# Modulation vectors of a two-block kernel: from multiply-adds on three engines to plain fp32 matmuls in four 32-column parts

## The chip, the cores and the metric

One Trainium2 chip, one NeuronCore, one launch. The metric is device microseconds of the launch; the kernel before took 2239.73 us (median of 3 runs, 2230.85 to 2242.94). The engines have separate instruction queues that run in order: PE (TensorE), DVE (VectorE), ACT (ScalarE), POOL (GpSimd) and SP, which here issues nearly all DMAs. SP's queue is in order too: a DMA that waits for its buffer holds up every DMA behind it.

## What is computed

The input runs through two layers of a first block (four mixer branches, gates, a feed-forward part) and then through two layers of a second block (attention, gating, convolution, a feed-forward part with 22 tiles of 128 hidden units). Each layer `l` of the second block needs six modulation rows of 1024 numbers, for the latent stream (from `c`) and for the context stream (from `c_ctx`):

```python
def adaln(cvec, w, b, n):
    m = jax.nn.silu(cvec) @ w[:, : n * D_MODEL] + b[: n * D_MODEL]
    return jnp.split(m, n, axis=-1)

cmod = adaln(c_ctx, w_mod[l], b_mod[l], 2 if last else 6)
...
sh1, sc1, g1, sh2, sc2, g2 = [m[:, None, :] for m in adaln(c, w_mod[l], b_mod[l], 6)]
```

`w_mod[l]` is 1024 x 6144 in fp32, 25.2 MB a layer. It depends on nothing that the blocks compute, so it may be done at any time before its layer. In the last layer the context stream needs two of the six rows only.

## The kernel before

The large projections are done as three fp32r matmuls each (`mm3`, L509 to L511): weights are loaded as 512 KB units into a ring of six buffers (`RAW = 6`, tag "raw", L262), split by ACT into `hi` (L275) and by DVE into `lo` (L278), at most four split units ahead of PE (`HL = 4`).

The modulation vectors are made by a generator, `mods(l)`, that is advanced in small steps by `fill(n)` beside other work. A step takes one unit of 512 KB of `w_mod`: two slabs of 128 rows by 512 columns. There are 48 steps a layer: six rows `r`, two halves `h` of 512 columns, four pairs of slabs. The units are loaded on SP (L1133) into the same ring of six buffers as the other weights, one unit ahead (`WM_AHEAD = 1`).

In a step each slab is multiplied by one number per partition of silu(c) (and of silu(c_ctx) where that is needed) and added to an accumulator `macc` of 128 x 512. The first slab is written by ACT (L1151). For the latent stream DVE does a fused multiply-add (L1156). For the context stream ACT multiplies the slab in place (L1153) and POOL adds it (L1154). After four steps the 128 partitions of `macc` are summed by PE with a one-hot stationary operand `pick` (L1164): plain fp32, four matmuls per stream, each on a 32-column part of the array, with 128 moving columns. DVE copies the sums out of PSUM (L1167), PE transposes them (L1169), DVE adds the bias (L1171). For rows 2 and 5 the resulting columns are written to DRAM from POOL's queue with 4-byte elements (L1175, tile `md`), and read back later as rows (L1180).

The steps are taken in five stages: 16 in the gate part of the first block's layer 0 (one in every second gate unit), 22 in its feed-forward part (one per hidden tile), 10 in the feed-forward part of the first block's layer 1, and for the second layer's vectors 33 and 15 in the two parts of the feed-forward of the second block's layer 0 (three per hidden tile, 512 tokens). The order of instructions on each engine is fixed when the program is made, by a list scheduler that goes by priorities in program order and a timeline of its own; buffers are packed into memory by the same program.

Of the kernel before, what the change touches and what calls it, by code (L numbers as in the profile page):

```python
# [9 lines left out]
F32 = mybir.dt.float32  # L10
FR = mybir.dt.float32r
AF = mybir.ActivationFunctionType
# [17 lines left out]
KEEP = 962 + 4 + 2 * (280 + 80 + 96 + 48)  # L30
# [268 lines left out]
class Kern:  # L299
# [8 lines left out]
    MPOOL = (1,)  # L308
# [14 lines left out]
    WM_AHEAD = 1  # L323
# [7 lines left out]
    def __init__(self, nc, tc, ctx, dr, stop=None):  # L331
# [15 lines left out]
        self.ident, cst, self.tabs, self.pick, self.ct, self.ones, self.nh, self.par_f = (  # L347
            self.keep(n) for n in (128, cpk.n, 512, 64, 16, 1, 1, 240))
# [246 lines left out]
    # ---------------------------------------------------------------- first block  # L595
# [515 lines left out]
    # ---------------------------------------------------------------- second block  # L1111
    def mods(self, l):
        nc, dr = self.nc, self.dr
        if l == 0:
# [12 lines left out]
        units = [(r, h, k) for r in range(6) for h in range(2) for k in range(0, 8, 2)]  # L1127
        loaded = []

        def load():  # L1130
            r, h, k = units[len(loaded)]
            wm = self.wp.tile([128, UNIT], F32, tag="raw", name=f"wm{l}_{r}_{h}_{k}", bufs=self.RAW)
            nc.sync.dma_start(wm, dr["w_mod"][l, r, h, k // 2])  # L1133
            loaded.append(wm)

        for i, (r, h, k0) in enumerate(units):
# [3 lines left out]
            if h == 0 and k0 == 0:  # L1140
                col = self.keep(16).rearrange("p (w m) -> p w m", w=2)
                self.mcol[l, r] = col
            if k0 == 0:
                acc = self.slot("macc")
            for k in (k0, k0 + 1):
                w = loaded[i][:, 512 * (k - k0):512 * (k - k0) + 512]
                for which in range(nw):
                    c = self.ct[:, 2 * k + which:2 * k + which + 1]
                    dst = acc[:, 512 * which:512 * which + 512]
# [7 lines left out]
            if k0 < 6:  # L1157
                yield
                continue
# [640 lines left out]
```

## Time and profile before

| | |
|---|---|
| median of 3 runs | 2239.73 us |
| profiled execution: span | 2238.6 us |
| mean granted TensorE clock | 0.973 |
| PE busy (matmul records) | 2101.8 us, 94% |
| DVE / ACT / POOL busy | 1575.9 / 1175.6 / 681.8 us |
| DMA read from HBM | 361.8 MB, mean 163 GB/s |

The page is of one execution. PE's busy time is a union of matmul records, whose ends are modelled and overlap, so 94% hides slow stretches: in a stretch without waits 256-column fp32r matmuls start 0.12 us apart though each record lasts 0.28 us. What the modulation steps cost is read by setting stages with such steps beside equal stages without, and by the waits inside them. A plain fp32 matmul has two records on PE.

### The profile page before, as it was taken

To read this page: it belongs to the slowest core of one execution; us is meant where nothing else is said; L and a number is where in the kernel's file an instruction comes from. 1 tells how busy PE (TensorE), PEld (TensorE's weight loads), DVE (VectorE), ACT (ScalarE), POOL (GpSimd) and SP (SyncE) were. 2 spreads that over 40 slices of the span, in tenths; PEclk is the share of its full clock that TensorE was granted. 3 is DMA by queue.
4 is the path that set the end of the run, shared out by engine and by line. 5 is a ranking of instruction groups with operands and counts; after the bars stand their busy time and mean duration, and the time that the engine had idled before them with its cause. 6 is when DMAs were issued, how large, how long until landed. Compare 5 with 4: busy or idle time off the path is not lost.

```text
span 2238.6 us, 34899 instructions
## 1 busy us (share of the span) xinstructions
PE 2101.8 (94%) x13152; PEld 1824.3 (81%) x13152; DVE 1575.9 (70%) x2594; ACT 1175.6 (53%) x2084; POOL 681.8 (30%) x564
## 2 busy tenths in 40 slices
PE   8999999976999999999897997998989999899999
PEld 7788898876888888998887886686778888678997
DVE  8757788856669566758985569779856635976664
ACT  6456756645554555556665455556323334465552
POOL 2102243556513100212545217109411221721330
PEclk9999999988999999999998999899999999999999
DMA  7545566676755444456567654245745722324553
GB/s 269 182 139 164 158 206 207 192 145 213 232 184 179 160 134 140 141 180 207 171 139 154 235 169 149 78 149 172 204 150 179 170 85 85 113 85 142 182 195 113
DMA packets 102552, 366.70 MB, mean 164 GB/s; under 512 B 12752, under 2 KB 12912, under 8 KB 102384
## 3 DMA queue, kind: packets, MB, share of 16 engines
q1 hardware_dynamic: 99920, 358.65, 52.1%
q0 software_dynamic: 2464, 5.83, 1.0%
q8 instruction: 103, 1.69, 0.3%
q14 instruction: 65, 0.53, 0.1%
HBM read 361.76 MB, written 2.68 MB: 163 GB/s over the span
## 4 chain that ended last, share of the span: by engine, by line
PE 72%; DVE 13%; DMA 5%; issue 5%; POOL 4%; ACT 2%; SPq 0%; DVEq 0%; POOLq 0%; ACTq 0%
PE mm L509 21%; PE mm L510 21%; PE mm L511 21%; DMA wm<-in_w_mod 4%; DVE lo L278 4%; DVE cv L1482 3%; POOL macc L1154 3%; DVE macc L1156 2%; PE ax L1292 1%; ACT hi L275 1%; PE ax L932 1%; PE ax L891 1%; DMA raw<-in_w_f 1%; PE ax L1320 1%; PE ax L890 1%
## 5 line engine op out<-in xcount | busy, mean ns | idle before, releaser
L278 DVE TENSOR_TENSOR lo<-raw,hi 128x1024 fp32r<-128x1024 f32 (+2 forms) x552 | 741.5, 1346 | 379.4 <-ACT hi L275 376.4
L275 ACT ACTIVATE hi<-raw 128x1024 fp32r<-128x1024 f32 (+1 forms) x564 | 593.2, 1053 | 620.7 <-PE mm L510 252.6
L509 PE MATMUL mm<-hThi,hi 128*128 128x256 f32 (+1 forms) x2408 | 730.2, 305 | 8.7 <-DVE gz L1271 2.9
L511 PE MATMUL mm<-hThi,lo 128*128 128x256 f32 (+1 forms) x2408 | 724.3, 302 | 9.1 <-DVE lo L278 9.1
L510 PE MATMUL mm<-hTlo,hi 128*128 128x256 f32 (+1 forms) x2408 | 727.3, 303 | 0.5 <-DVE hTlo L472 0.5
L509 PEld LDWEIGHTS mm<-hThi,hi 128*128 128x128 f32 x2408 | 466.2, 194 | 40.6 <-issue 13.1
L511 PEld LDWEIGHTS mm<-hThi,lo 128*128 128x128 f32 x2408 | 466.7, 194 | 26.2 <-DVE lo L278 9.3
L510 PEld LDWEIGHTS mm<-hTlo,hi 128*128 128x128 f32 x2408 | 467.9, 194 | 17.3 <-issue 3.3
L1154 POOL TENSOR_TENSOR macc<-macc,wm 128x512 f32<-128x512 f32 x112 | 191.2, 1708 | 179.7 <-ACT wm L1153 170.3
L1156 DVE SCALAR_TENSOR_TENSOR macc<-wm,kept,macc 128x512 f32<-128x512 f32 x168 | 182.8, 1088 | 70.1 <-DMA wm<-in_w_mod 57.4
L510 PE MATMUL mm<-lo,hThi 128*128 128x512 f32 (+2 forms) x480 | 182.1, 380 | 9.7 <-DVE lo L278 9.7
L509 PE MATMUL mm<-hi,hThi 128*128 128x512 f32 (+2 forms) x480 | 181.7, 386 | 5.5 <-DVE rb L580 3.1
L511 PE MATMUL mm<-hi,hTlo 128*128 128x512 f32 (+2 forms) x480 | 180.2, 378 | 0.0
L509 PE MATMUL mm<-hi,hh 128*128 128x512 f32 x440 | 172.4, 392 | 0.0
L510 PE MATMUL mm<-lo,hh 128*128 128x512 f32 x440 | 172.0, 391 | 0.0
L511 PE MATMUL mm<-hi,hl 128*128 128x512 f32 x440 | 171.7, 391 | 0.0
L839 POOL TENSOR_TENSOR th<-th,gh 128x512 f32<-128x512 f32 (+1 forms) x44 | 54.4, 1237 | 262.6 <-DVE th L1533 262.6
L1153 ACT ACTIVATE wm<-wm,kept 128x512 f32<-128x512 f32 x112 | 80.1, 721 | 77.0 <-DVE macc L1156 74.3
L510 PEld LDWEIGHTS mm<-lo,hThi 128*128 128x128 f32 x480 | 90.9, 190 | 27.9 <-DVE lo L278 12.4
L509 PEld LDWEIGHTS mm<-hi,hThi 128*128 128x128 f32 x480 | 90.8, 190 | 27.7 <-issue 8.5
L511 PEld LDWEIGHTS mm<-hi,hTlo 128*128 128x128 f32 x480 | 90.4, 189 | 16.6 <-issue 0.7
L511 PEld LDWEIGHTS mm<-hi,hl 128*128 128x128 f32 x440 | 83.0, 189 | 17.6
(354 smaller groups left out, 3189.2 us busy)
## 6 DMA issues: line engine op xcount, KB each, us to landing
raw<-in_w_f SPq DMA_DIRECT2D x364, 512.0 KB, 4.1
raw<-in_w_s SPq DMA_DIRECT2D x190, 512.0 KB, 3.5
wm<-in_w_mod SPq DMA_DIRECT2D x96, 512.0 KB, 4.3
bc<-csd POOLq DMA_DIRECT2D x32, 128.0 KB, 4.3
mrow<-md SPq DMA_DIRECT2D x6, 512.0 KB, 3.9
row<-in_rows SPq DMA_DIRECT2D x4, 512.0 KB, 4.9
raw<-in_w_f SPq DMA_DIRECT2D x4, 510.0 KB, 4.7
par<-in_par_s SPq DMA_DIRECT2D x2, 918.5 KB, 8.0
```

Of the source, the lines that this page charges most:

```text
L275: nc.scalar.activation(hi[:, :n], raw[:, :n], AF.Copy)
L278: ins = eng.tensor_sub(lo[:, :n], raw[:, :n], hi[:, :n].bitcast(F32)).ins
L509: nc.tensor.matmul(ps, ah, bh, start=first, stop=False)
L510: nc.tensor.matmul(ps, ah, bl, start=False, stop=False)
L511: nc.tensor.matmul(ps, al, bh, start=False, stop=last)
L839: nc.gpsimd.tensor_mul(tt, tt, gh)
L890: nc.tensor.matmul(ps[:, 0:128], q[:, :128], k[:, :128], start=True, stop=True)
L891: nc.tensor.matmul(ps[:, 128:384], q[:, 128:], k, start=True, stop=True)
L1153: nc.scalar.activation(w, w, AF.Copy, scale=c)
L1154: nc.gpsimd.tensor_add(dst, dst, w)
L1156: nc.vector.scalar_tensor_tensor(dst, w, c, dst, op0=ALU.mult, op1=ALU.add)
L1482: nc.vector.scalar_tensor_tensor(c, y[:, j:j + 256], wj, c, op0=ALU.mult, op1=ALU.add)
```

## The change

`mods` no longer multiplies on DVE, ACT and POOL. A padded stationary operand `ctp` (128 x 32 for each of eight 128-row blocks, silu(c) and silu(c_ctx) in columns 0 and 1, zeros in the rest) is made once. `w_mod` is laid out on the host as units of 128 rows x 1024 columns of one row `r`: still 48 units of 512 KB a layer, one per (`r`, 128-row block `k`). Every second step (`MSTEP = 2`) PE does two blocks: for each, four plain fp32 matmuls with 256 moving columns, one on each 32-column part of the array, all accumulating in one PSUM tile over the eight blocks. Then ACT copies 128 x 256 out, PE transposes twice, DVE adds the bias to eight columns at once. The units have a ring of their own of four buffers (tag "wm", `WM = 4`), and are loaded two steps ahead. Rows 2 and 5 are still written to DRAM from POOL's queue, now with one DMA of 1024 4-byte elements per stream instead of two of 512.

```diff
-            nc.gpsimd.memset(self.pick, 0.0)
-            nc.gpsimd.memset(self.pick[:, 0:1], 1.0)
-            nc.gpsimd.memset(self.pick[:, 33:34], 1.0)
+            nc.gpsimd.memset(self.ctp, 0.0)
+            nc.vector.tensor_copy(self.ctp.rearrange("p (k m) -> p k m", k=8)[:, :, 0:2], self.ct.rearrange("p (k w) -> p k w", k=8))
...
-            wm = self.wp.tile([128, UNIT], F32, tag="raw", name=f"wm{l}_{r}_{h}_{k}", bufs=self.RAW)
+            wm = self.wp.tile([128, UNIT], F32, tag="wm", name=f"wm{l}_{r}_{k}", bufs=self.WM)
...
-            while len(loaded) <= min(47, i + self.WM_AHEAD):
+            while len(loaded) <= min(47, i + self.MSTEP):
                 load()
...
-                    if k == 0:
-                        nc.scalar.activation(dst, w, AF.Copy, scale=c)
-                    elif which in self.MPOOL:
-                        nc.scalar.activation(w, w, AF.Copy, scale=c)
-                        nc.gpsimd.tensor_add(dst, dst, w)
-                    else:
-                        nc.vector.scalar_tensor_tensor(dst, w, c, dst, op0=ALU.mult, op1=ALU.add)
...
+            if (k + 1) % self.MSTEP:
                 yield
                 continue
+            for kk in range(k + 1 - self.MSTEP, k + 1):
+                for j in range(4):
+                    nc.tensor.matmul(ps[32 * j:32 * j + 32, :256], self.ctp[:, 32 * kk:32 * kk + 32],
+                                     loaded[i - k + kk][:, 256 * j:256 * j + 256], start=kk == 0, stop=kk == 7,
+                                     skip_group_check=True, tile_position=(0, 32 * j))
+            if k < 7:
+                yield
+                continue
+            mo = self.tmp("mo", 256)
+            nc.scalar.activation(mo, ps[:, :256], AF.Copy)
             ps = self.ax_ps("am")
...
+            for e in range(2):
+                nc.tensor.transpose(ps[:, 128 * e:128 * e + 128], mo[:, 128 * e:128 * e + 128], self.ident)
...
-                    nc.gpsimd.dma_start(md[which, r // 3, 512 * h:512 * h + 512].rearrange("(j p) -> p j", p=128), col[:, which, o])
+                    nc.gpsimd.dma_start(md[which, r // 3, :].rearrange("(j p) -> p j", p=128), col[:, which, :])
             yield
```

## Rows read from the trace of the kernel before

**Rows 1.** The page, part 4: the ending chain by line, share of the span.

```profile
PE mm L509 21%; PE mm L510 21%; PE mm L511 21%; DMA wm<-in_w_mod 4%; DVE lo L278 4%; DVE cv L1482 3%; POOL macc L1154 3%; DVE macc L1156 2%; PE ax L1292 1%; ACT hi L275 1%; PE ax L932 1%; PE ax L891 1%; DMA raw<-in_w_f 1%; PE ax L1320 1%; PE ax L890 1%
```

**Rows 2.** Stages: stretch, us; busy PE, PEld, DVE, ACT, POOL; clock; DMA share; GB/s.

```profile
1501.00:1637.00 136.00, 118.34 (x556) 91.20 (x555) 117.44 (x121) 64.87 (x93) 81.25 (x50) 0.95 0.62 189
1708.00:1819.00 111.00, 111.00 (x514) 90.09 (x513) 68.58 (x83) 41.21 (x53) 33.33 (x22) 1.00 0.61 160
2057.00:2175.00 118.00, 118.00 (x988) 117.78 (x987) 76.63 (x106) 67.15 (x106) 36.36 (x41) 1.00 0.59 189
420.00:593.00 173.00, 134.73 (x1080) 130.02 (x1079) 114.05 (x111) 91.88 (x154) 111.36 (x81) 0.88 0.71 192
1086.00:1255.00 169.00, 147.97 (x1162) 139.31 (x1161) 129.34 (x199) 93.25 (x204) 82.25 (x72) 0.93 0.66 162
195.00:376.00 181.00, 175.16 (x1411) 160.56 (x1411) 147.24 (x234) 115.07 (x212) 74.88 (x53) 0.99 0.58 188
849.00:1018.00 169.00, 169.00 (x1346) 157.53 (x1346) 109.31 (x197) 93.57 (x176) 28.11 (x25) 1.00 0.48 152
```

**Rows 3.** The page's costliest groups: the two accumulating lines.

```profile
L1154 POOL TENSOR_TENSOR macc<-macc,wm 128x512 f32<-128x512 f32 x112 | 191.2, 1708 | 179.7 <-ACT wm L1153 170.3
L1156 DVE SCALAR_TENSOR_TENSOR macc<-wm,kept,macc 128x512 f32<-128x512 f32 x168 | 182.8, 1088 | 70.1 <-DMA wm<-in_w_mod 57.4
```

**Rows 4.** What PE waited for in the stretch 420 to 593: total us, times, longest.

```profile
PE am L1164 <- DVE macc L1156: 20.8, 5, 13.4
PE mm L511 <- DVE lo L278: 9.1, 1, 9.1
PE am L1164 <- POOL macc L1154: 8.4, 4, 3.0
```

**Rows 5.** PE in order of time around one set of 32-column matmuls, full clock.

```profile
1762.52 0.39 PE L509 MATMUL mm<-hThi,hi 128*128 128x512 f32 x1
1762.75 0.39 PE L510 MATMUL mm<-hTlo,hi 128*128 128x512 f32 x1
1763.07 0.43 PE L1164 MATMUL am<-macc,kept 128*32 128x128 f32 x8
1763.42 0.50 PE L511 MATMUL mm<-hThi,lo 128*128 128x512 f32 x1
```

**Rows 6.** Tile `am`: the 32-column records; min, median, max ns.

```profile
L1164 PE MATMUL am<-macc,kept x320: 269/297/423, 218.0 to 1763.2; 128*32 128x128 f32 x160
```

**Rows 7.** Matmul groups by shape: a plain fp32 one with 256 columns.

```profile
L932 PE MATMUL ax<-pt,fv 128*64 128x256 f32 x32 | 10.3, 405 | 0.0
```

**Rows 8.** What PE waited for over the whole span: the copy ahead of the transpose.

```profile
PE am L1169 <- DVE mo L1167: 11.0, 5, 4.4
```

**Rows 9.** Tile `wm`: idle time of the engines that read it, by what ended it.

```profile
  DMA wm<-in_w_mod: 68.8, 22
```

**Rows 10.** Tile `md`: its DMAs on POOL's queue.

```profile
L1175 POOL DMA_DIRECT2D md<-kept x12: 750/792/837, 452.2 to 1769.7; - x12
```

**Rows 11.** Stretches right behind `md` writes, columns as in rows 2.

```profile
454.00:472.00 18.00, 10.91 (x91) 10.70 (x90) 8.07 (x8) 5.81 (x10) 11.81 (x8) 0.91 0.57 26
491.00:507.00 16.00, 12.26 (x103) 12.06 (x101) 4.85 (x5) 4.64 (x8) 3.63 (x4) 0.98 0.95 33
1609.00:1616.00 7.00, 7.00 (x33) 5.73 (x32) 5.75 (x9) 3.89 (x6) 2.15 (x3) 1.00 0.79 35
```

**Rows 12.** PE, DVE and ACT in order of time around the first of these stretches.

```profile
464.63 0.28 PE L510 MATMUL mm<-hTlo,hi 128*128 128x256 f32 x1
478.32 0.66 PE L1164 MATMUL am<-macc,kept 128*32 128x128 f32 x8 [13.42 <-DVE macc L1156]
...
476.73 1.54 DVE L1156 SCALAR_TENSOR_TENSOR macc<-wm,kept,macc 128x512 f32<-128x512 f32 x2 [14.64 <-DMA wm<-in_w_mod]
...
474.18 1.06 ACT L275 ACTIVATE hi<-raw 128x1024 fp32r<-128x1024 f32 x1 [13.35 <-DMA raw<-in_w_f]
```

**Rows 13.** What PE waited for in the stretch 1086 to 1255.

```profile
PE ax L1310 <- DVE dp L1303: 11.9, 2, 10.0
```

More of the change, by code (lines that the diff above doesn't have):

```diff
@@ L29 @@
          for n in ns.split()}
-KEEP = 962 + 4 + 2 * (280 + 80 + 96 + 48)
+KEEP = 1154 + 4 + 2 * (280 + 80 + 96 + 48)
 LIM = 2.4e19
@@ L322 @@
     SIDE2 = 5
-    WM_AHEAD = 1
+    MSTEP = 2
+    WM = 4
     HL = 4
@@ L346, in __init__ @@
         self.kept, self.kept_n = kept, 0
-        self.ident, cst, self.tabs, self.pick, self.ct, self.ones, self.nh, self.par_f = (
-            self.keep(n) for n in (128, cpk.n, 512, 64, 16, 1, 1, 240))
+        self.ident, cst, self.tabs, self.ctp, self.ct, self.ones, self.nh, self.par_f = (
+            self.keep(n) for n in (128, cpk.n, 512, 256, 16, 1, 1, 240))
         self.cst_all, self.cst = cst, {n: cpk.get(cst, n) for n in cpk.at}
@@ L1126, in mods @@
         self.md[l] = md
-        units = [(r, h, k) for r in range(6) for h in range(2) for k in range(0, 8, 2)]
+        units = [(r, k) for r in range(6) for k in range(8)]
         loaded = []
         def load():
-            r, h, k = units[len(loaded)]
-            wm = self.wp.tile([128, UNIT], F32, tag="raw", name=f"wm{l}_{r}_{h}_{k}", bufs=self.RAW)
-            nc.sync.dma_start(wm, dr["w_mod"][l, r, h, k // 2])
+            r, k = units[len(loaded)]
+            wm = self.wp.tile([128, UNIT], F32, tag="wm", name=f"wm{l}_{r}_{k}", bufs=self.WM)
+            nc.sync.dma_start(wm, dr["w_mod"][l, r, k])
@@ L1134, in load @@
             loaded.append(wm)
-        for i, (r, h, k0) in enumerate(units):
+        for i, (r, k) in enumerate(units):
             nw = 2 if l == 0 or r < 2 else 1
-            while len(loaded) <= min(47, i + self.WM_AHEAD):
+            while len(loaded) <= min(47, i + self.MSTEP):
                 load()
[L1140 to L1149, printed above, removed]
-                    if k == 0:
-                        nc.scalar.activation(dst, w, AF.Copy, scale=c)
-                    elif which in self.MPOOL:
-                        nc.scalar.activation(w, w, AF.Copy, scale=c)
-                        nc.gpsimd.tensor_add(dst, dst, w)
-                    else:
-                        nc.vector.scalar_tensor_tensor(dst, w, c, dst, op0=ALU.mult, op1=ALU.add)
-            if k0 < 6:
@@ L1158, in mods @@
+            if k == 0:
+                ps = self.ax_ps("am")
+            if (k + 1) % self.MSTEP:
                 yield
                 continue
-            ps = self.ax_ps("am")
-            for which in range(nw):
-                for j in range(4):
-                    o = 512 * which + 128 * j
-                    nc.tensor.matmul(ps[32 * j:32 * j + 32, :128], self.pick[:, 32 * which:32 * which + 32], acc[:, o:o + 128],
-                                     start=which == 0, stop=which == nw - 1, skip_group_check=True, tile_position=(0, 32 * j))
@@ new lines, in mods @@
+            if k < 7:
[3 more added lines that the diff above has]
+            nc.scalar.activation(mo, ps[:, :256], AF.Copy)
+            ps = self.ax_ps("am")
+            for e in range(2):
+                nc.tensor.transpose(ps[:, 128 * e:128 * e + 128], mo[:, 128 * e:128 * e + 128], self.ident)
+            col = self.keep(16).rearrange("p (w m) -> p w m", w=2)
+            self.mcol[l, r] = col
+            nc.vector.tensor_add(col[:, :nw, :].rearrange("p w (j e) -> p w j e", e=2),
+                                 ps[:, :256].rearrange("p (e j m) -> p m j e", e=2, m=32)[:, :nw],
+                                 bm[:, 8 * r:8 * r + 8].rearrange("p (j e) -> p j e", e=2)[:, None].to_broadcast([128, nw, 4, 2]))
```

11 lines of the change are left out of this document (1 added, 10 removed).

## The prediction

> **What bounds the kernel now.** I read the chain that ended last first: the three lines of split matmuls hold 63% of the span, and the modulation steps appear as waits between them, for the load of `wm` (4%) and for the two accumulating lines (3% and 2%) [rows 1]. So PE is the bound, and the steps cost where PE stands still for them or slows after it. How much is read from stages [rows 2]. The feed-forward part of 22 hidden tiles without steps (from 2057) took 118 us at full clock; the same 22 tiles with 22 steps (from 420) took 173 us at clock 0.88: 55 us more. The gate part with 16 steps (from 195) took 181 us, the same part a layer later without steps (from 849) 169: 12 more. The two parts of the second block's feed-forward have equal work and took 136 us with 33 steps and 111 with 15; eleven tiles of 512 tokens at the matmul spacing of 0.227 us (1762.52 to 1762.75, [rows 5]) make 48 matmuls x 0.227 = 10.9 us each, so ten intervals from first to last tile are 109: 27 and 2 us of loss. The stage from 1086 with 10 steps took 169 us where 118 are feed-forward; of its 51 us a part is attention that runs beside it, and 10 of them one stall of PE behind DVE [rows 13].
>
> In the worst stage the waits are for the accumulators, 20.8 us for DVE's and 8.4 for POOL's, and 9.1 once for a weight split [rows 4]. The longest, 13.4 us, is not arithmetic: PE started nothing from 464.63 to 478.32, DVE stood 14.6 us waiting for a `wm` load, ACT 13.4 us for a weight load [rows 12]. In the stretch 454 to 472 the DMA engines moved 26 GB/s, where the stage's mean is 192 [rows 2, 11]. It begins 2 us after POOL issued the `md` writes with 4-byte elements at 452 [rows 10]. A pair of such writes was followed by 16 to 18 us of this, a single one by 7 [rows 11]: about 8.3 us per write of 512 elements, 12 writes in all.
>
> **Removed.** 183 us of DVE and 191 us of POOL work [rows 3], ACT's scaling, and their waits. On PE the 32-column sums go: 320 records are 40 sets of eight [rows 6]. One set held the next matmul off from 1762.98 (1762.75 plus a spacing) to 1763.42, 0.44 us [rows 5]; 40 of them are 18 us, which lie inside the stage losses above. The 24 transposes stay.
>
> **Added on PE.** What one set tells: eight records end within 0.43 us while one lasts 0.297 [rows 5, 6], so the four parts do run at once, and the second half of the fp32 product starts 0.43 - 0.297 = 0.13 us after the first. A plain fp32 record with 256 columns lasts 0.405 us [rows 7], as long as the fp32r one with 512 [rows 5], so it streams 512 columns' time, 0.227 us, plus the 0.02 by which 0.13 exceeds half of that: 0.25 us a half. A step does two blocks of two halves: 4 x 0.25 = 1.0 us, and getting in and out costs what the old set shows beyond its two halves, 0.44 - 0.26 = 0.18. That is 1.18 us for each of 48 steps (96 units taken in pairs), 57 us. Lower bound: streaming alone, 4 x 0.227 x 48 = 44. Upper bound: the whole set of 0.44 us scaling with columns and blocks, 1.76 x 48 = 84. I take 57, since set and record are the same form. Each of 12 tails waits for a copy and transposes; old tails cost 11.0 us of PE wait [rows 8], so at most 0.9 each; I take 0.5 to 0.8.
>
> [...]
>
> **Moved.** PE's queue is in order and now waits for the `wm` load itself; behind a late one every projection matmul waits. The loads run two steps ahead in a ring of their own of four, and the weight ring keeps all six buffers, which it shared before. The six buffers and four split units are some 9 units of 24 matmuls x 0.12 us, 2.9 us each (3.2 with the steps): 27 to 30 us in which PE can live without DMA.
>
> The `md` writes keep their number of elements but bunch up: for the first layer's rows 2 and 5, 2 writes of 1024 each at one time instead of two separate pairs of 512. By 8.3 us per 512 that is one stretch of 33 us for two of 17; for the second layer one of 17 for two of 8. So the cover counts once. DVE, POOL and SP have no other step moved past them; the copy on ACT (128 x 256, 12 times) and the one-time fill of `ctp` are priced at nothing beside ACT's 53% and POOL's idle time; uncovered they would be under 10 us. The accumulating PSUM tile is now held over eight steps instead of a moment; no row shows a wait for a bank, so it is priced at nothing, with the 11.9 us that PE waited inside the attention [rows 13] as its bound to either side.
>
> **The sum, stage by stage (change of the loss).**
> - Gate part: 8 x 1.18 + 2 x 0.8 = 11 for 12: -1 (-4 to +4).
> - Feed-forward from 420: 11 x 1.18 = 13, 2 for tails, some 18 for the long stretch and the slow clock after it, 4 for the rest: 37 for 55, -18. Bounds: with cover for all but 5 us of the stretch -32; with `wm` late from the fourth unit behind it (four fills of 6.3 us after the last step) 20 us of stall and more slow clock, -8.
> - From 1086: 5 x 1.18 + 1 is 7, the second long stretch 6 to 10 beyond its cover; against them the 10 us stall [rows 13], six sets (2.6) and slow clock (0.93 of 169 us, some 10): -8 (-18 to +6).
> - Second block, first part: 16.5 x 1.18 = 19, tails 3, stretch 3: 25 to 27 for 27: 0 (-5 to +8).
> - Second part: 7.5 x 1.18 + 1 = 10 for 2: +8 (+6 to +12). Here DVE had hidden the steps, and PE cannot.
>
> Together -19: 57 us of matmuls are paid to remove about 80 us of sets, waits and slow clock. The span of 2238.6 becomes 2219.6; the median of the runs lies 1.1 us above the span, so the time is 2220 us.
>
> **The rivals.**
> 1. The gain is eaten (2239 less 4, 2235). The bunched writes starve PE as long as the two pairs did: the stage from 420 gains 8 instead of 18, that from 1086 gains 3. For it: the 13 us stall in [rows 12] began 10 us into its stretch, so much less than 27 us of weights were ahead. Against: `wm` units then sat in the weight ring.
> 2. Slower: waits for `wm` stand in PE's own queue. DVE and ACT waited 68.8 us for it in 22 waits [rows 9]; before, part of that was hidden because PE went on. If all of it falls on PE, it replaces the some 21 us that I gave to the stretches: -19 + 48 = +29, 2268 us. It decides from 41 us of such waits on, where the gain is gone. For it: in order queue, two units needed at once, DMA share 0.71 in that stage [rows 2]. Against: own ring, earlier loads.
> 3. All waits go. If the six weight buffers cover the long stretches too, what is left is 57 + 8 us of PE work for 12 + 55 + 20 + 27 + 2 = 116 us of losses (20 being the modulation's share of the 51): -51, 2188 us.
> 4. The change doesn't do what it says: the parts run one after another with 256 columns. Then 768 records x 0.25 us = 192 us for 57, 135 more: 2355 us. Against it stand the eight records in 0.43 us [rows 5].
>
> [...]
>
> **How the numbers follow.** Forecast (2208 to 2229): 0.41. Rival 1 (2229 to 2251): 0.25. Rival 3: 0.16. Rival 2: 0.15. Rival 4: 0.03. About 0.5%, 11 us, is what a measurement of this kernel can tell. Faster than 2228.5: nearly all of the forecast and rival 3, 0.57. Within 0.5%: rival 1 and the edges, 0.25. Slower: rivals 2 and 4, 0.18. The range leaves out the fastest part of rival 3 and the slowest of rivals 2 and 4: 2196 to 2260.
>
> **What would show it.** In the profile after: sixteen records of a step within 1.2 us of PE (rival 4: over 3.5); the stage from 420 at 150 to 160 us with clock above 0.93; one DMA stretch of about 33 us below 50 GB/s behind each of the first layer's two `md` bursts; the second part from 1708 at about 119 us; PE's waits for `wm` under 25 us in sum. I am wrong if a step costs over 1.6 us, if waits for `wm` pass 41 us, or if the weight ring shows no more cover than before.

## The result and the profile after

The changed kernel takes 2186.54 us (median of 4 runs, 2180.66 to 2187.76) where the kernel before takes 2236.39 (4 runs, 2230.85 to 2242.94): ratio 0.9753, 95% interval 0.9721 to 0.9784, 50 us faster. Forecast were 2220 us and a range of 2196 to 2260, so the time lies below the range, next to the value that the third rival had (2188).

The profiled execution of after has a span of 2184.1 us against 2238.6. From its page, part 1 (busy time and instructions of each engine):

```profile
PE 2120.3 (97%) x13600; PEld 1822.1 (83%) x13600; DVE 1365.4 (63%) x2391; ACT 1087.8 (50%) x1944; POOL 477.4 (22%) x444
```

And part 4 (the ending chain by line, as in [rows 1]):

```profile
PE mm L509 27%; PE mm L510 26%; PE mm L511 26%; PE am L1146 2%; DVE cv L1471 2%; PE ax L1281 1%; DVE lo L278 1%; PE ax L932 1%; PE ax L891 1%; PE ax L890 1%; PE ax L1309 1%; PE ay L462 1%; PE ay L591 1%; ACT hi L275 1%; PE ax L1299 0%
```

The three projection lines hold 79% of the chain instead of 63%. The load of `wm` (4% in [rows 1]) and both accumulating lines (3% and 2%) are gone from it, and in their place stands 2% for the new matmuls (L1146). PE is busy 18 us longer in a span that is 54 shorter: the time came out of its idle time, 136.8 us before (2238.6 - 2101.8) and 63.8 now.

The stages, with the columns of [rows 2], each from its first to its last tile as there. They stand in order of time: gate part, feed-forward part with steps, the first block's second feed-forward, both parts of the second block's feed-forward, and the feed-forward without steps:

```profile
203.00:385.00 182.00, 182.00 (x1467) 161.44 (x1466) 110.43 (x200) 92.57 (x176) 27.59 (x24) 1.00 0.56 184
431.00:569.00 138.00, 130.53 (x1110) 125.19 (x1108) 60.55 (x67) 63.57 (x107) 43.50 (x44) 0.96 0.69 209
1066.00:1213.00 147.00, 144.62 (x1155) 134.62 (x1154) 98.37 (x175) 82.24 (x182) 53.16 (x53) 0.99 0.62 178
1460.00:1574.00 114.00, 114.00 (x628) 87.95 (x628) 51.39 (x58) 41.27 (x55) 31.51 (x21) 1.00 0.56 192
1649.00:1765.00 116.00, 116.00 (x570) 92.58 (x569) 57.18 (x53) 41.27 (x53) 28.61 (x21) 1.00 0.38 123
2003.00:2120.00 117.00, 117.00 (x981) 116.88 (x980) 76.57 (x105) 66.18 (x104) 36.35 (x41) 1.00 0.60 189
```

Set against [rows 2], with the forecast beside it:

| stretch | before, us | after, us | change | forecast |
|---|---|---|---|---|
| start to first gate unit | 195 | 203 | +8 | 0 |
| gate part | 181 | 182 | +1 | -1 |
| feed-forward with steps | 173 | 138 | -35 | -18 |
| first block, second feed-forward | 169 | 147 | -22 | -8 |
| second block, first part | 136 | 114 | -22 | 0 |
| second block, second part | 111 | 116 | +5 | +8 |
| feed-forward without steps | 118 | 117 | -1 | 0 |
| all between these | 1155.6 | 1167.1 | +11.5 | 0 |
| span | 2238.6 | 2184.1 | -54.5 | -19 |

Three stages give back 79 us where 26 were expected, and 19.5 are lost where none was expected: 8 ahead of the first gate unit, the rest between the stages. The two belong together. Of the steps' 768 records 218 lie ahead of the first gate unit or between the stages (the 60 of one such gap are below). That is 13.6 of the 48 steps, and they hold PE for over 20 us there, while the forecast had paid for all 48 inside the stages. So some 16 us of the 79 (13.6 x 1.18) are work that moved, and not a loss that went.

In the worst stage PE's idle time (span less busy) fell from 38.3 us to 7.5, that is 31 of its 35. The other 4 are busy time: the new matmuls are 7.3 us of it, the old sums were 5.0, and the rest, some 6 us less, goes with the clock, 0.88 before and 0.96 now. Over the whole span the mean granted clock went from 0.973 to 0.990. The traces show two granted levels, 1.00 and 0.50; in after 256-column fp32r matmuls start 0.213 us apart at 0.50 (starts from 492.69 to 496.75) and 0.12 at 1.00 (from 497.15 on). So a mean of c is a share 2 x (1 - c) of the time at the lower level, 121 us before and 44 us after, and each such microsecond of running matmuls costs 0.44 of itself (1 - 0.12 / 0.213): up to 34 us of the gain are clock.

The steps themselves. PE in order of time around two steps that stand one behind the other:

```profile
1701.72 0.39 PE L510 MATMUL mm<-hTlo,hi 128*128 128x512 f32 x1
1701.95 0.39 PE L511 MATMUL mm<-hThi,lo 128*128 128x512 f32 x1
1702.27 1.93 PE L1146 MATMUL am<-wm,kept 128*32 128x256 f32 x32
1704.13 0.50 PE L509 MATMUL mm<-hThi,hi 128*128 128x512 f32 x1
```

From 1701.95 to 1704.13 are 2.18 us, less the spacing of 0.23: 1.95 for two steps of 16 records. Taken one by one in the same way over the whole trace, a lone step holds PE 1.09 us. But the scheduler has broken many up: the 768 records stand in 70 groups where 48 steps were written, 18 of them are lone steps of 16 records, and a group of two records already holds PE 0.64 us. All groups together hold it for some 66 us. Inside one the four parts start 7 ns apart and the two halves of the fp32 product 0.22 to 0.24 us apart, where 512 columns stream in 0.227: the parts are as good as free. The records of the steps by stretch (first PE column; sixteen records are one step), for the second block's first part, the gap behind it and the start of the program:

```profile
1460.00:1574.00 114.00, 11.77 (x176) 5.00 (x176) 1.00 0.56 192
1574.00:1649.00 75.00, 4.06 (x60) 1.74 (x60) 1.00 0.42 140
0.00:203.00 203.00, 7.12 (x56) 1.94 (x56) 1.00 0.61 210
```

Eleven steps lie in that first part and some four in the gap behind it; three and a half run before the first gate unit, where the first set of the kernel before comes at 218 [rows 6].

What PE waited for over the whole span (us in total, times, longest):

```profile
PE ay L462 <- DVE xs L458: 8.1, 4, 2.7
PE mm L510 <- DVE lo L278: 7.6, 5, 2.5
PE mm L510 <- issue: 5.5, 1, 5.5
PE am L1146 <- DMA wm<-in_w_mod: 2.3, 1, 2.3
```

Tile `wm`, idle time of its reader, as in [rows 9]:

```profile
  DMA wm<-in_w_mod: 4.8, 2
```

And what SP's queue waited for longest:

```profile
SPq L1132 <- PE am L1146: 107.7, 48, 6.0
```

PE's waits for `wm` are 2.3 us (4.8 of idle time for the tile, against 68.8 in [rows 9]). SP waits 107.7 us for one of the four `wm` buffers, but its queue holds 0% of the ending chain.

Tile `md`, its DMAs on POOL's queue, as in [rows 10]:

```profile
L1164 POOL DMA_DIRECT2D md<-kept x6: 888/942/982, 470.3 to 1709.9; - x6
```

The stretches behind them, with the columns of [rows 2]: the first layer's two pairs, then two single writes of the second layer.

```profile
472.00:493.00 21.00, 13.53 (x111) 12.35 (x110) 4.14 (x5) 5.41 (x9) 4.58 (x5) 0.85 0.54 26
1147.00:1156.00 9.00, 9.00 (x78) 9.00 (x77) 4.54 (x6) 5.06 (x12) 2.54 (x3) 1.00 0.37 26
1550.00:1561.00 11.00, 11.00 (x60) 8.40 (x59) 3.38 (x6) 3.44 (x5) 3.64 (x2) 1.00 0.21 34
1712.00:1721.00 9.00, 9.00 (x41) 7.48 (x40) 4.68 (x5) 2.52 (x4) 2.77 (x2) 1.00 0.17 27
```

Twice the elements in one burst gave 21 us and not 33 behind the first pair. Behind the second the rate rose again after 9 us and fell once more (76 GB/s from 1146 to 1167), and PE was busy throughout. Behind the first PE ran for 13.5 of the 21 and stood still for most of the rest in one piece (PE in order of time):

```profile
490.82 0.37 PE L510 MATMUL mm<-hTlo,hi 128*128 128x256 f32 x1 [5.46 <-issue]
```

From 486.9 to 497.1 its clock was at the lower level, 0.50.

### The profile page after: what moved, and what is told of

Same layout as the page of the kernel before. It is cut to its first block, busy times and chain, and to the rows that moved or that the text cites. A ratio compares the mean times of both kernels' runs of the same rounds, so it can differ in the third digit from the quotient of the medians.

```text
span 2184.1 us, 35036 instructions
## 1 busy us (share of the span) xinstructions
PE 2120.3 (97%) x13600; PEld 1822.1 (83%) x13600; DVE 1365.4 (63%) x2391; ACT 1087.8 (50%) x1944; POOL 477.4 (22%) x444
## 4 chain that ended last, share of the span: by engine, by line
PE 90%; DVE 6%; issue 1%; ACT 1%; DMA 1%; SPq 0%; POOL 0%; DVEq 0%; ACTq 0%
PE mm L509 27%; PE mm L510 26%; PE mm L511 26%; PE am L1146 2%; DVE cv L1471 2%; PE ax L1281 1%; DVE lo L278 1%; PE ax L932 1%; PE ax L891 1%; PE ax L890 1%; PE ax L1309 1%; PE ay L462 1%; PE ay L591 1%; ACT hi L275 1%; PE ax L1299 0%
## 5 line engine op out<-in xcount | busy, mean ns | idle before, releaser
L278 DVE TENSOR_TENSOR lo<-raw,hi 128x1024 fp32r<-128x1024 f32 (+2 forms) x552 | 717.1, 1301 | 553.8 <-ACT hi L275 547.9
L511 PE MATMUL mm<-hThi,lo 128*128 128x256 f32 (+1 forms) x2408 | 717.1, 299 | 0.0
L509 PEld LDWEIGHTS mm<-hThi,hi 128*128 128x128 f32 x2408 | 460.5, 192 | 50.3 <-issue 20.0
L511 PEld LDWEIGHTS mm<-hThi,lo 128*128 128x128 f32 x2408 | 462.0, 192 | 21.0 <-issue 7.0
L510 PEld LDWEIGHTS mm<-hTlo,hi 128*128 128x128 f32 x2408 | 463.0, 192 | 17.6 <-issue 4.1
L839 POOL TENSOR_TENSOR th<-th,gh 128x512 f32<-128x512 f32 (+1 forms) x44 | 48.9, 1110 | 310.3 <-DVE th L1522 310.3
L509 PEld LDWEIGHTS mm<-hi,hh 128*128 128x128 f32 x440 | 82.6, 188 | 17.8 <-ACT hi L275 0.8
L510 PEld LDWEIGHTS mm<-lo,hh 128*128 128x128 f32 x440 | 82.6, 188 | 17.1
L1471 DVE SCALAR_TENSOR_TENSOR cv<-yp,kept,cv 128x256 f32<-128x256 f32 x120 | 87.6, 736 | 2.5 <-ACT cv L1467 0.7
```

The costliest lines, as they stand in the source:

```text
L278: ins = eng.tensor_sub(lo[:, :n], raw[:, :n], hi[:, :n].bitcast(F32)).ins
L509: nc.tensor.matmul(ps, ah, bh, start=first, stop=False)
L510: nc.tensor.matmul(ps, ah, bl, start=False, stop=False)
L511: nc.tensor.matmul(ps, al, bh, start=False, stop=last)
L839: nc.gpsimd.tensor_mul(tt, tt, gh)
L1471: nc.vector.scalar_tensor_tensor(c, y[:, j:j + 256], wj, c, op0=ALU.mult, op1=ALU.add)
```

## The experiments

Theories. The chain theory: slab arithmetic on three engines cost much more than the waits that name it, because DVE and ACT also make the split weights that PE needs; taking it off gives the gain. The burst theory: the `md` stretches carry the gain (fewer bursts, better covered). The ring theory: `wm` units no longer take weight buffers. The order theory: the matmuls of after cost little because the scheduler is free to move them. The numbers of the labels give the order in which they were run. A ratio is always against the kernel before, measured on the same chip.

### What the slab arithmetic cost: e1, e10, e11, e14, e13

**e1.** Before, with all slabs after the first left out of the sums (their loads, sets, tails and `md` writes stay).

```diff
-                    elif which in self.MPOOL:
-                        nc.scalar.activation(w, w, AF.Copy, scale=c)
-                        nc.gpsimd.tensor_add(dst, dst, w)
                     else:
-                        nc.vector.scalar_tensor_tensor(dst, w, c, dst, op0=ALU.mult, op1=ALU.add)
+                        nc.scalar.activation(dst[:, k:k + 1], w[:, 0:1], AF.Copy, scale=c)
```

> The kernel before with the scaling and adding of every slab after the first left out (one element of each slab is still read, so that the loads and their order stay); the sums on PE, the copies and the writes of md stay as they are. The modulation vectors are therefore not those of the reference. Theory 'chain' (PE loses most by waiting for ACT, DVE and POOL at the accumulators, and by the half clock behind each wait): 60 to 75 us less than before, about 2165 to 2175, clock near 0.99. Theory 'DMA' (most was lost in the stretches behind the md writes and by the shared ring): less than 25 us, above 2211, with the stall of 13 us behind the first md write still there.

Measured: 2150.54 us against 2229.66, ratio 0.9637 (0.9604 to 0.967): 80 us less. The stages of [rows 2] from 420, from 1086 and the second block's first part:

```profile
415.00:557.00 142.00, 131.47 (x1077) 127.62 (x1076) 61.15 (x74) 81.89 (x189) 46.54 (x46) 0.93 0.82 233
1051.00:1199.00 148.00, 141.56 (x1141) 134.32 (x1140) 97.59 (x178) 88.16 (x212) 52.65 (x55) 0.97 0.68 181
1436.00:1545.00 109.00, 107.47 (x546) 85.54 (x545) 51.96 (x68) 62.54 (x146) 29.99 (x22) 1.00 0.71 231
```

They are 31, 21 and 27 us shorter than in [rows 2], and they are the same three stages in which after gained. The arithmetic on its own cost 80 us, more than the chain theory said, with the small `md` writes and the shared ring still there. The two routes of this arithmetic were then taken away one at a time.

**e10.** Before, without the context stream's 112 scalings on ACT and 112 adds on POOL (left out of the sums).

```diff
                     elif which in self.MPOOL:
-                        nc.scalar.activation(w, w, AF.Copy, scale=c)
-                        nc.gpsimd.tensor_add(dst, dst, w)
+                        pass
```

> The kernel before without the context stream's scaling on ACT and adding on POOL (112 of each; modulation vectors are not the reference's); DVE's 168 multiply-adds stay. Of the 80 us that e1 gained by leaving out both: if the chain through ACT and POOL holds PE back, 45 to 65 us less than before; if DVE's does (28 us of PE's wait were put down to it, 11 to POOL's), 15 to 30 us less.

**e11.** Before, without the latent stream's 168 multiply-adds on DVE (left out; ACT reads one element instead).

```diff
-                        nc.vector.scalar_tensor_tensor(dst, w, c, dst, op0=ALU.mult, op1=ALU.add)
+                        nc.scalar.activation(dst[:, k:k + 1], w[:, 0:1], AF.Copy, scale=c)
```

> The kernel before without the latent stream's 168 multiply-adds on DVE (one element of each slab is read by ACT instead; modulation vectors are not the reference's); ACT's scaling and POOL's adding stay. If DVE's chain holds PE back: 45 to 65 us less than before; if ACT's and POOL's does: 15 to 30 us less. If the two are each other's cover, both e10 and e11 gain little (under 20 us) and only leaving out both gains.

Measured: e10 2165.27 us against 2236.28, ratio 0.9678 (0.9637 to 0.972), 71 less; e11 2189.99, ratio 0.9789 (0.9745 to 0.9834), 46 less. The sum, 117, is more than the 80 of both, so each route was dear because of the other. DVE's part alone costs 80 - 71 = 9 us, ACT's and POOL's alone 80 - 46 = 34, both together 80 (the 9 and the 34 are differences of two runs, uncertain by some 12 us to either side). In [rows 4] the waits of PE said the opposite: 20.8 us for DVE's line, 8.4 for POOL's. The e11 figure has a flaw of its own: the one-element copy that stands in for DVE's work is in ACT's queue, and PE waits for it over the span of e11,

```profile
PE am L1164 <- ACT macc L1156: 32.2, 7, 14.8
```

so the 46 may be less than DVE's multiply-adds cost, and the 34 more than ACT's and POOL's part.

**e14.** Before, with the context stream's slabs added by DVE as well: 280 multiply-adds there, none on POOL, the whole computation done.

```diff
-    MPOOL = (1,)
+    MPOOL = ()
```

> The kernel before with the context stream's slabs added by DVE too (112 more multiply-adds of about 0.75 us, 84 us of DVE work) and none on ACT's scaling and POOL. If the chain over three engines costs: 30 to 60 us less than before, though DVE works more. If the amount of work beside the weight split costs: within 15 us of before, or slower.

Measured: 2196.53 us against 2235.79, ratio 0.9809 (0.9769 to 0.9849), 39 less, though DVE has 112 more instructions. The page's groups of DVE's multiply-adds, in e14 and then in e10 (busy time and mean ns):

```profile
L1156 DVE SCALAR_TENSOR_TENSOR macc<-wm,kept,macc 128x512 f32<-128x512 f32 x280 | 235.1, 873 | 48.2 <-DMA wm<-in_w_mod 37.6 <-ACT macc L1151 10.3
```

```profile
L1155 DVE SCALAR_TENSOR_TENSOR macc<-wm,kept,macc 128x512 f32<-128x512 f32 x168 | 149.2, 889 | 56.9 <-DMA wm<-in_w_mod 49.4 <-ACT macc L1151 6.1
```

The same instruction takes 873 or 889 ns without POOL's adds and 1088 with them [rows 3]. The weight split, which DVE does for every unit of weights, tells the same; its group in e14 and in e11, where POOL adds and DVE doesn't:

```profile
L278 DVE TENSOR_TENSOR lo<-raw,hi 128x1024 fp32r<-128x1024 f32 (+2 forms) x552 | 710.2, 1289 | 365.6 <-ACT hi L275 363.2
```

```profile
L278 DVE TENSOR_TENSOR lo<-raw,hi 128x1024 fp32r<-128x1024 f32 (+2 forms) x552 | 738.6, 1341 | 538.1 <-ACT hi L275 529.1
```

Single instructions show it best. DVE in order of time in one stretch of e11:

```profile
421.63 1.23 DVE L278 TENSOR_TENSOR lo<-raw,hi 128x1024 fp32r<-128x1024 f32 x1 [1.46 <-ACT hi L275]
...
429.86 3.67 DVE L278 TENSOR_TENSOR lo<-raw,hi 128x1024 fp32r<-128x1024 f32 x2
433.90 1.87 DVE L278 TENSOR_TENSOR lo<-raw,hi 128x1024 fp32r<-128x1024 f32 x1
```

And POOL in the same stretch:

```profile
420.41 0.73 POOL L839 TENSOR_TENSOR tt<-tt,gh 128x256 f32<-128x256 f32 x1
424.48 6.29 POOL L1154 TENSOR_TENSOR macc<-macc,wm 128x512 f32<-128x512 f32 x4
430.73 1.73 POOL L839 TENSOR_TENSOR tt<-tt,gh 128x256 f32<-128x256 f32 x1
432.42 4.51 POOL L1154 TENSOR_TENSOR macc<-macc,wm 128x512 f32<-128x512 f32 x2
```

With POOL idle a split takes 1.23 us; beside POOL's work it takes 1.84 (mean of two) and 1.87. POOL's own 128 x 256 product takes 0.73 us with DVE idle and 1.73 beside a split. Each slows the other; through what, no run shows.

**e13.** Before, with ACT's scaled slab in a buffer of its own (two of them) instead of in place. The rival to the reading above: DVE must have read `wm` before ACT may write over it, and that order is what costs.

```diff
-                        nc.scalar.activation(w, w, AF.Copy, scale=c)
-                        nc.gpsimd.tensor_add(dst, dst, w)
+                        ws = self.tp.tile([128, 512], F32, tag="tws", name=self.nm("ws"), bufs=2)
+                        nc.scalar.activation(ws, w, AF.Copy, scale=c)
+                        nc.gpsimd.tensor_add(dst, dst, ws)
```

> The kernel before, with ACT writing the scaled slab of the context stream to a tile of its own (two buffers) instead of over the slab, so that it need not wait until DVE has read it. All work stays. If the order of the engines on one slab costs: 25 to 50 us less than before. If the amount of work does: within 10 us.

Measured: 2238.27 us against 2235.79, ratio 0.9997 (0.9969 to 1.0025). DVE's multiply-adds stay slow:

```profile
L1157 DVE SCALAR_TENSOR_TENSOR macc<-wm,kept,macc 128x512 f32<-128x512 f32 x168 | 193.2, 1151 | 65.9 <-DMA wm<-in_w_mod 53.0 <-ACT macc L1151 11.4
```

So the order in place is not what cost. Another rival stays: ACT's 112 scalings, 80.1 us of work on the page of the kernel before, leave together with POOL's adds in e10 and in e14, and no run takes off one without the other. What is shown is the price of the route ACT and POOL, and that DVE's instructions are shorter without it.

### The `md` bursts: e2, e3, e8

**e2.** Before, with the `md` writes bunched as in after: once per row and stream, 1024 elements.

```diff
-                if r in (2, 5):
-                    nc.gpsimd.dma_start(md[which, r // 3, 512 * h:512 * h + 512].rearrange("(j p) -> p j", p=128), col[:, which, o])
+                if r in (2, 5) and h == 1:
+                    nc.gpsimd.dma_start(md[which, r // 3, :].rearrange("(j p) -> p j", p=128), col[:, which, :])
```

> The kernel before, with row 2 and row 5 written to md once per stream after the second half, 1024 elements in one write, instead of 512 after each half: that part of the change alone. If a write costs by its elements (8.3 us of slow DMA per 512, as forecast): the stretch behind a pair is 33 us, no gain, 2230 to 2250. If it costs by the write (about 10 us whatever its length): half the slow time goes, 8 to 20 us less, 2216 to 2228.

Measured: 2216.27 us against 2229.66, ratio 0.9927 (0.9893 to 0.996), 13 less. The stretch behind a pair of 1024, and behind a single 1024 of the second layer:

```profile
478.00:496.00 18.00, 12.31 (x103) 12.10 (x101) 4.97 (x5) 4.79 (x8) 3.87 (x4) 0.90 0.47 26
1751.00:1759.00 8.00, 8.00 (x37) 6.64 (x36) 4.55 (x4) 2.96 (x4) 2.32 (x2) 1.00 0.32 24
```

A pair of 1024 takes 18 us, as long as a pair of 512 in [rows 11]; a single 1024 takes 8 where a single 512 took 7. Halving the number of bursts halves the number of such stretches. Not every write slows the queues alike: behind the other single of e2 they moved 113 GB/s over 9 us, and behind three of the four singles of the kernel before 86 to 100 over 8. What the sum had as a cost (one stretch of 33 us) was a gain.

**e3.** After, with each of these writes split in two of 512 elements, one right behind the other.

```diff
-                    nc.gpsimd.dma_start(md[which, r // 3, :].rearrange("(j p) -> p j", p=128), col[:, which, :])
+                    for o in (0, 512):
+                        nc.gpsimd.dma_start(md[which, r // 3, o:o + 512].rearrange("(j p) -> p j", p=128), col[:, which, o // 128:o // 128 + 4])
```

> The kernel after, with each md write of 1024 elements split in two of 512, issued one behind the other. By elements: the slow stretches stay (20 us and 10 us), time 2183 to 2190. By the write: the stretch behind row 2 of the first layer grows from 20 to 33 to 40 us, PE's one stall there of 5.6 us to 18 or more, and the time goes up by 12 to 25 us, 2198 to 2212.

Measured: 2179.69 us, ratio 0.9762 (0.9734 to 0.9791), the same as after. Four writes instead of two, and the stretch is no longer:

```profile
472.00:490.00 18.00, 18.00 (x159) 17.28 (x158) 7.36 (x8) 7.41 (x12) 7.36 (x8) 1.00 1.00 40
```

So its length goes neither with elements nor with the number of writes, but with the burst: 7 to 11 us for one stream, 15 to 21 for two, at 512 or 1024 elements, but for the second pair of after, which was broken up after 9. Why is open.

**e8.** e5 (below) with `md` written as rows: from the copied sums, bias added there, four pieces of 1 KB per stream, in place of 1024 pieces of 4 bytes.

```diff
...
+                    nc.sync.dma_start(self.bmr.rearrange("(j m) n -> j m n", m=32)[:, which, :], dr["b_row"][l, r])
...
             nc.scalar.activation(mo, ps[:, :256], AF.Copy)
+            if r in (2, 5):
+                mr = self.tmp("mo", 256)
+                nc.vector.tensor_add(mr, mo, self.bmr)
+                for which in range(nw):
+                    nc.gpsimd.dma_start(md[which, r // 3, :].rearrange("(j n) -> j n", n=256),
+                                        mr.rearrange("(j m) n -> j m n", m=32)[:, which, :])
...
-                    nc.gpsimd.dma_start(md[which, r // 3, :].rearrange("(j p) -> p j", p=128), col[:, which, :])
```

> The kernel of e5 with rows 2 and 5 written to md from the copied sums, four pieces of 1 KB per stream, bias added beforehand by DVE, instead of 1024 4-byte elements. The slow stretches behind the writes should go altogether. If they still cost: the 5.6 us stall and 10 us of half clock behind the first write, and some at the others, 8 to 15 us less than e5. If the weight ring already covers them: within 4 us of e5.

Measured: 2166.97 us against 2236.76, ratio 0.9702 (0.9662 to 0.9743); beside e5 in the same runs 11.6 us less (2162.65 to 2177.9 against 2176.84 to 2184.61). The stretch behind the first layer's pair is gone:

```profile
468.00:488.00 20.00, 20.00 (x177) 19.15 (x179) 9.22 (x10) 9.14 (x16) 5.88 (x6) 1.00 0.71 243
```

243 GB/s at full clock, where after moved 26. Against e5 the stage from 420 gains nothing: both take 132 us there at full clock. The stage from 1086 gains 8 of the 11.6 us (147 for 155). In e5 the second pair's writes lie in it, and PE's one long wait:

```profile
PE mm L509 <- issue: 6.1, 1, 6.1
```

In e8 that wait is gone. Where the other 3.6 us come from was not followed, and after, with small pieces, also has 147 in this stage with PE busy through its second burst, so not every burst costs PE time. All queues together moved 26 GB/s behind the 4-byte writes of after and 243 behind the 1 KB ones here: a DMA of tiny pieces can slow all other queues. Through what, the traces do not show. Of the kernels that do the whole computation this is the fastest.

### The ring: e4, e9

**e4.** After, with the `w_mod` units back in the weights' ring of six.

```diff
-            wm = self.wp.tile([128, UNIT], F32, tag="wm", name=f"wm{l}_{r}_{k}", bufs=self.WM)
+            wm = self.wp.tile([128, UNIT], F32, tag="raw", name=f"wm{l}_{r}_{k}", bufs=self.RAW)
```

> The kernel after, with the w_mod units back in the weights' ring of six buffers instead of four of their own. If the own ring is what keeps PE from waiting for loads: 15 to 30 us more, PE's waits for wm above 20 us in sum. If not (theory 'chain'): within 8 us of after.

Measured: 2193.89 us, ratio 0.983 (0.98 to 0.986); 14 us above e3, which was measured beside it, and by the ratios 17 above after. PE's waits for `wm` grow, and stay far from the second rival's 41:

```profile
PE am L1146 <- DMA wm<-in_w_mod: 10.6, 4, 3.6
```

**e9.** Before, with `w_mod` in a ring of its own of two buffers.

```diff
-            wm = self.wp.tile([128, UNIT], F32, tag="raw", name=f"wm{l}_{r}_{h}_{k}", bufs=self.RAW)
+            wm = self.wp.tile([128, UNIT], F32, tag="wm", name=f"wm{l}_{r}_{h}_{k}", bufs=2)
```

> The kernel before, with the w_mod units in a ring of their own of two buffers (more of them don't fit beside its other buffers): the ring part of the change alone. If the own ring is worth what e4 says (sharing it cost the kernel after some 15 us): 10 to 18 us less than before. If in the kernel before the accumulators set the pace whatever the ring: within 6 us of before.

Measured: 2229.39 us against 2236.28, ratio 0.9967 (0.9946 to 0.9989), 7 less. Either way the own ring is worth some 7 to 14 us: a part of the gain, not its body. Before with a larger ring was not tried.

### The steps on PE: e5, e6, e7, e12

**e5.** After, with each step's matmuls held behind the projection matmul that precedes them in the program.

```diff
-            with self.behind():
+            with self.behind(), self.tc.issue_after(self.last_mm):
...
-        nc.tensor.matmul(ps, al, bh, start=False, stop=last)
+        self.last_mm = nc.tensor.matmul(ps, al, bh, start=False, stop=last).ins
```

> The kernel after, with every step's matmuls held behind the projection matmul that stands before the step in the program, so that the scheduler can't move them ahead into PE's waits. If the moving is part of the gain (768 records of which 56 ran before the first gate and others at the norms): 10 to 25 us more than after, ratio to before 0.98 to 0.987. If moving them costs (the first gate was reached 8 us later than before, with the DMA at 318 GB/s against 266 in the first 60 us): 5 to 10 us less, ratio 0.971 to 0.973. Neither: within 5 us.

Measured: 2178.6 us against 2236.76, ratio 0.9752 (0.9718 to 0.9785): after's own ratio. The feed-forward from 420 and both parts of the second block's:

```profile
422.00:554.00 132.00, 132.00 (x1171) 124.12 (x1170) 59.49 (x67) 64.14 (x110) 41.44 (x45) 1.00 0.78 251
1446.00:1564.00 118.00, 118.00 (x692) 89.19 (x691) 51.48 (x57) 41.47 (x56) 31.39 (x21) 1.00 0.64 221
1636.00:1755.00 119.00, 119.00 (x616) 94.08 (x615) 56.15 (x54) 41.59 (x54) 29.33 (x21) 1.00 0.42 142
```

The first starts 9 us earlier than in after, and the second block's parts, which now hold their own steps, are 4 and 3 us longer. The records of the steps stand in 50 groups and hold PE some 55 us, 11 less than in after, and nearly all of them lie in the stages that the forecast gave them. That the scheduler moves steps gains nothing and costs nothing that can be measured: the order theory falls. With eleven steps (176 records, 12 us) the feed-forward from 420 takes 132 us, 14 more than without steps, and PE never stands still in it: of the 55 us of loss nothing is left but the steps and their tails. e5 is the base of e6, e7, e8 and e12.

**e6.** e5 with every 32-column matmul done twice, with half the operand.

```diff
-            nc.vector.tensor_scalar(self.ct, th, 0.5, None, op0=ALU.mult)
+            nc.vector.tensor_scalar(self.ct, th, 0.25, None, op0=ALU.mult)
...
-            for kk in range(k + 1 - self.MSTEP, k + 1):
+            for kk, again in [(a, b) for a in range(k + 1 - self.MSTEP, k + 1) for b in range(2)]:
...
```

> The kernel of e5 with every 32-column matmul issued twice on half the stationary operand. A step of sixteen records held PE for 1.09 us in the kernel after. If the steps lie on the path: 48 more of them, with 1.0 us each since in and out are paid once, 45 to 55 us more than e5. If most of them fill waits of PE: less than 30 us. If parts ran one after another: over 100 us.

**e7.** e5 with the matmuls of every even block left out (their loads stay).

```diff
-            for kk in range(k + 1 - self.MSTEP, k + 1):
+            for kk in (k,):
...
```

> The kernel of e5 with the even 128-row blocks' matmuls left out (the modulation vectors are not the reference's); all units are still loaded. On the path: half a step less in 48, 0.45 us each, 20 to 25 us less than e5. In waits: less than 10 us.

Measured: e6 2208.74 us, ratio 0.9892 (0.9847 to 0.9937), 30 above e5; e7 2147.1, ratio 0.9607 (0.957 to 0.9644), 32 below e5. A step of e6 holds PE 1.95 us, so 48 x 0.86 = 41 were added and 30 reached the end. A set of eight, as each step of e7 is, holds PE 0.66, so 48 x 0.43 = 21 were taken and 32 came back. The two do not agree in size: e6 added 96 sets of eight and paid 0.31 us for each, at the edge of what was expected if most steps filled waits; e7 took 48 and got 0.66 for each back, more than PE had held for them. So the steps lie on the path for the larger part, and their price is known only as some 38 us (three quarters of 48 x 1.09, from e6) to 64 (twice e7's 32), with the forecast's 57 inside. A serial execution of the four parts was expected to add over 100 in e6, and it did not.

**e12.** e5 with one block per step: 96 sets of eight in place of 48 of sixteen.

```diff
-    MSTEP = 2
+    MSTEP = 1
...
-            while len(loaded) <= min(47, i + self.MSTEP):
+            while len(loaded) <= min(47, i + 2):
```

> The kernel of e5 with one 128-row block per step instead of two (MSTEP = 1, loads still two ahead): twice as many entries into the 32-column parts. A set of eight records held PE for 0.66 us where sixteen held it for 1.09: 48 x (2 x 0.66 - 1.09) = 11 us more than e5 if the steps lie on the path; within 4 us if not, or if the scheduler joins them again.

Measured: 2181.62 us against 2236.28, ratio 0.975 (0.9704 to 0.9795); e5 had 0.9752. The scheduler joined many of the sets again: the records stand in 77 groups, where 96 were written and e5 has 50. By the trace they hold PE some 8 us longer than in e5, not the 48 x (2 x 0.66 - 1.09) = 11 of the expectation, and nothing of it is seen in the time; the intervals are too wide to exclude it.

## Why the prediction was wrong

**Right: the price and the form of a step.** Forecast 1.18 us, measured 1.09 for a step in one piece (all 70 groups of after hold PE 66 us for the 57 of the sum, the 50 of e5 55); the four parts run at once, so the fourth rival (one after another) is out. Halves are 0.22 to 0.24 us apart, for the 0.25 of the sum and a stream of 0.227: the parts overlap in full. That the steps lie on PE's path held for the larger part of their price (e6, e7).

**Right: the second rival stays away.** PE's waits for `wm` are 2.3 us, the mark was 25 for "right" and 41 for "wrong". Even in the shared ring they are 10.6 (e4).

**Right in the second part and the gate part:** +5 for +8 and +1 for -1, and with the steps held in place (e5) +8 and -2.

**Wrong: what was kept of the old losses.** This is the step that failed. The sum priced the new work per stage and then kept a residue of the loss: 18 us of stretch and slow clock and 4 "for the rest" from 420, 6 to 10 for the second long stretch, 3 for tails and 3 for a stretch in the second block's first part. With the arithmetic off DVE, ACT and POOL the residues went too. From 420 the loss is now 138 - 118 = 20: seven steps (112 records) are 7.6, PE's idle time 7.5, and a clock of 0.96 over 138 us, that is 11 us at the lower level, in part while PE stood, at most 5. e1 shows it without the new matmuls: 80 us from the arithmetic alone, where the sum removed "about 80" of sets, waits and slow clock all told and still wanted the bunched bursts to take some of it back. The first part shows it best: 27 us were kept as steps, tails and stretch, and what is there is eleven steps, 12 us, PE busy for all 114. e5 has the steps where the sum had them: 132, 155, 118 us from 420, from 1086 and in the first part, for 155, 161 and 136 forecast. These three differences, 47 us, make up the miss: forecast was a span of 2219.6, and that of e5 is 2175.0.

**Wrong: where that loss was looked for.** It was read from PE's waits by the name that ended them last: 20.8 us for DVE, 8.4 for POOL [rows 4]. POOL's adds hardly showed there, yet without them and ACT's scalings for them 71 us go (e10), and with DVE doing them in addition to its own 39 (e14). Beside them the weight splits and the multiply-adds that PE does wait for were longer (a split 1.84 to 1.87 us for 1.23 in e11, a multiply-add 1088 ns on average for 889 in e10). The signs stood in the rows: 1088 ns on average for DVE's multiply-add and 1708 for POOL's add [rows 3]. They were taken as the price of those instructions, not as something that could vary.

**Wrong: the `md` burst.** Priced at 8.3 us per 512 elements it gave 33 us; it is 21 behind the first pair and 9, then a second dip, behind the other, and as bursts became fewer the change gained on this (e2: 13 us in the kernel before). [rows 11] had three of the eight stretches, and of the single writes the slowest one alone.

**Wrong: slow clock.** It entered only inside those residues, and with some 10 us from 1086. By the granted clock of the three stages before (0.88, 0.93, 0.95) they held 42, 24 and 14 us at the lower level; after (0.96, 0.99, 1.00) 11, 3 and 0. PE's idle time in these stages went from 38.3, 21.0 and 17.7 us to 7.5, 2.4 and 0: with PE's stalls the slow clock went too.

**Wrong: the base of the second block.** The two parts were said to have equal work. Without the steps' records after has 628 - 176 = 452 in the first and 570 - 84 = 486 in the second. Counted by shape and spacing the first has some 4 us less of matmuls in the kernel before and 9 less in after, so its loss before was over 30 and not 27.

**Not seen: 19.5 us outside the stages.** The first gate unit is reached 8 us later, and the stretches between the stages are longer by 11.5. It is the steps themselves that lie there, 13.6 of them: the forecast kept every step in its stage. The 56 records ahead of the first gate unit hold PE 7 us; in e4 and e5 none lies there, and the unit is reached at 195 and 199 us.

**The third rival had the value, not quite the way.** It said that all waits go and 65 us of PE work stay. The waits went nearly so. But the stretch from 472 still cost PE some 10 us (7.5 idle, and 0.44 of the 6 in which it ran at the lower clock), and the steps held PE 66 us and not 57; that the sum still comes out means that more than its 116 us of old losses went, as in the first part above. Its chance of 0.16 was too low for a case in which a bound was already known from the clean part: the feed-forward without steps had 118 us with nothing kept.

**A balance from the runs.** Arithmetic -80 (e1), bursts -13 (e2), ring -7 to -14 (e9, e4), old sets 40 x 0.44 = -18, steps +38 to +64 (e6, e7): -54 to -87 for a measured -50. The terms come from different kernels and overlap, so they need not add; the balance shows what is large and what is small, and no more.

**Open.** How POOL's adds turn into 71 us: the slowing of DVE's instructions is shown, by means and by single instructions, but a chain from each slowed split to a stall of PE was not followed, and ACT's scaling went with the adds in e10 and e14. By what means DVE and POOL slow each other. What sets the length of a burst. Why e6 and e7 give such different prices for a set. Doubled or halved steps without the hold of e5 were not tried.

## What to carry to other kernels

Where helper engines are charged with waits, don't keep a residue of the loss by names: take as one bound the same stage without the helper work, and ask what the removed instructions did to those of other engines beside them (a split took 1.23 us alone and 1.84 to 1.87 beside POOL's adds), because that doesn't appear under their name. Work for the engine that is the bound can be worth adding if its price per step is known to a tenth of a microsecond (1.09 us here), and more so where the stage with the stalls also ran at a lower clock (0.88 in the worst one here, 0.96 after). And where a transfer of tiny pieces stands behind a stall, its layout is the next thing to mend: 1 KB pieces were worth 11.6 us here, though not every burst of tiny pieces had stopped PE.

## What the runs showed of the hardware

- DVE and POOL slow each other: a split 1.23 us alone and 1.84 to 1.87 beside POOL's adds, POOL's 128 x 256 product 0.73 alone and 1.73 beside a split, the multiply-add 873 to 889 ns on average without POOL's adds and 1088 with them. Giving 112 of the adds to POOL, with a scaling on ACT for each, made the kernel 39 us slower than leaving them on DVE (e14).
- Behind a DMA of 1024 pieces of 4 bytes all queues together moved 24 to 34 GB/s for 8 to 11 us in three of four stretches measured (113 in the fourth), behind two at a time, in the stretches shown, 26 to 40 for 18 to 21 us, with one pair at 26 for only 9. Neither elements nor the number of writes set the length. With 1 KB pieces the first pair's stretch moved 243 GB/s.
- Four 32-column parts in plain fp32 overlap in full: 16 records with 256 columns take 1.09 us, eight take 0.66, and two to four, where the scheduler had split a block, still 0.64.
